# A four-layer encoder trunk on one core: the on-chip buffers get new addresses

## The chip, the core and the metric

One core of a Trainium2 chip runs the whole kernel. TensorE (PE) multiplies and writes to PSUM, VectorE (DVE), ScalarE (ACT) and GpSimd (POOL) do the rest, and SyncE's queue (SP) issues the transfers from HBM into SBUF, the on-chip memory of 128 partitions in which every tile lies at one byte address in each partition. The metric is the device time of one execution in microseconds. The kernel before takes 2548.47 us (median of 3 runs, 2547.91 to 2550.18).

## The reference

Input is x of 512 frames by 1024 features in float32. Four layers follow (FoX attention, mLSTM, gMLP, FoX), each with a SwiGLU behind it, and a last RMSNorm.

```python
def swiglu(h, w_gu, w_down):
    g, u = jnp.split(h @ w_gu, 2, axis=-1)
    return (jax.nn.silu(g) * u) @ w_down

def reference(x, norm1_g, norm2_g, final_g, ...):
    for i in range(DEPTH):
        kind, j = i % N_MIXERS, i // N_MIXERS
        hn = rmsnorm(x, norm1_g[i])
        if kind == 0:
            y = forgetting_attention(hn, a_w_in[j], a_b_f[j], a_w_out[j])
        elif kind == 1:
            y = mlstm_mixer(hn, ...)
        else:
            y = gmlp_mixer(hn, ...)
        x = x + y
        x = x + swiglu(rmsnorm(x, norm2_g[i]), ffn_w_gu[i], ffn_w_down[i])
    return rmsnorm(x, final_g)
```

SwiGLU has 2816 inner features, 22 tiles of 128. FoX has 16 heads of 64 with softmax over all earlier frames, mLSTM 8 heads of 128 with a short convolution ahead of it, gMLP 2048 gated features.

## The kernel before

The residual stream stays in SBUF as eight tiles X[k] of 128 features by 512 frames. Each operand of a large product is split into an exact high and a low part in float32r (`split`, lines 119 and 120: ACT rounds to the high part, DVE takes the difference), and each product runs as three passes (`mm3`, lines 124 to 126): high weights by high input, high weights by low input, low weights by high input. Three such matmuls of 128x512 are called a triple here. The stationary operand is loaded anew for each matmul. In `dense` the 128x128 slice of the weights (wH, wL) is stationary and the activation tile moves through the array: h = x * g (hH, hL) for the gate and up products of SwiGLU and the q, k, o and u products of the mixers, the activations aH, aL for SwiGLU's down projection, and the mixers' results oH, oL for their output products (`out_steps`). In `quarter_steps` (lines 164 to 166) and `token_major` (343 to 345), which make v with frames on partitions, the weights move and h is stationary.

There are 1984 triples with h (1408 of SwiGLU, 576 of the mixers), 704 with a, and 320 with o (64 of each FoX, 64 of mLSTM, 128 of gMLP). SwiGLU goes through its 22 tiles in groups of 8, 8 and 6: two products with h for each tile, then eight down products with the group's activations. Nothing else is put between those products. In the mixers `weave` puts the steps of the products with h, v and the first output products between the small matmuls of the heads (scores s from kk and qq, transposes pt, products po); the last four o tiles of a mixer have their output product behind all heads, with nothing between.

Tiles are handed out by pools that lie one behind the other in SBUF, in the order in which they are opened, and a tag with a number of buffers goes round them; a new tile waits until the old one in its place has been read. Weights come in units of 128x1024 into raw (3 buffers) and are split into wH and wL (4 buffers each). Pools opened inside a stage (fox, mlstm, gmlp, swiglu) take the room behind the standing ones and give it back. The order of the instructions on each engine is made by the scheduler of the language, so it can shift with the pools.

Of the kernel before, what the change touches and what calls it, by code (L numbers as in the profile page):

```python
# [16 lines left out]
P = 128  # L17
S = 512
# [12 lines left out]
# columns of the packed per-partition constants  # L31
# [7 lines left out]
class Trunk:  # L39
    """The residual stream is kept feature-major, X[k] = [128 features, 512 frames]. Every  # L40
    large product runs as three float32r passes over exact high and low parts."""

    def __init__(self, ctx, tc, a, first_g, first_w):
# [3 lines left out]
        pool = lambda name, **kw: ctx.enter_context(tc.tile_pool(name=name, **kw))  # L47
        self.cp = pool("const", bufs=1)
        self.xp = pool("resid", bufs=1)
        self.hp = pool("hid", bufs=1)  # L50
        self.wp = pool("wts", bufs=4)
        self.np_ = pool("norm", bufs=1)
# [5 lines left out]
        # the first weights come in quarters, between the k-tiles of x  # L58
# [22 lines left out]
        # mask[q, 384 + k] = 0 where q >= k, else NEG, and 0 in the columns before  # L81
# [25 lines left out]
    def weights_tiles(self):  # L107
        return (self.wp.tile([P, 1024], F32, name=self.nm("raw"), tag="raw", bufs=3),
                self.wp.tile([P, 1024], F32R, name=self.nm("wH"), tag="wH", bufs=4),
                self.wp.tile([P, 1024], F32R, name=self.nm("wL"), tag="wL", bufs=4))  # L110

# [22 lines left out]
    def dense_steps(self, src, xs, done):  # L134
        """The same product as a list of steps, to be woven with other work."""
# [13 lines left out]
    def quarter_steps(self, src, done):  # L149
        """256 columns, frames on partitions: src [2][128, 4 k-tiles * 256]."""  # L150
# [21 lines left out]
    def out_steps(self, src, o, final=False):  # L172
        """X += (4 k-tiles of o, which fills by the time of emission) @ w."""
# [16 lines left out]
    def start(self, steps, product, at=KT - 2):  # L190
        """The first quarter of v, k-tile by k-tile as they come, and RMSNorm's sums."""
# [26 lines left out]
    def norm_k(self, k):  # L218
        """X[k] is final: its part of h (whole for the last norm) and its squares."""
        if self.next_g == C_GF:  # L220
            self.squares_k(k)
            self.hidden_k(k)
        else:
            self.hidden_k(k)
            self.squares_k(k)
# [18 lines left out]
    def squares_k(self, k, pool=None):  # L244
        """Sums of squares; with a pool for them, in two sums on two engines."""
# [48 lines left out]
    def swiglu(self, l):  # L294
        nc = self.nc
        with ExitStack() as es:
            fp = es.enter_context(self.tc.tile_pool(name="ffn", bufs=2, reuse_waits="tile"))
            for k0, kn in FGROUPS:
                acts = []
                for j in range(k0, k0 + kn):  # L300
# [17 lines left out]
                    hi = fp.tile([P, S], F32R, name=self.nm("aH"), tag="aH", bufs=10)  # L318
                    lo = fp.tile([P, S], F32R, name=self.nm("aL"), tag="aL", bufs=10)
# [9 lines left out]
    def token_major(self, src, then=None):  # L329
        """src [4 units][128, 2 k-tiles * 512]; returns 4 PSUM tiles [128 frames, 512]."""  # L330
# [17 lines left out]
    def logsig(self, y, t):  # L348
        """y = log_sigmoid(y) = min(y, 0) - ln(1 + exp(-|y|))"""
# [8 lines left out]
    def fox(self, j):  # L358
        with ExitStack() as es:
            pool = lambda name, **kw: es.enter_context(  # L360
                self.tc.tile_pool(name=name, reuse_waits="tile", **kw))
            kp = pool("a_keep", bufs=1)
# [32 lines left out]
            # steps a (scores, softmax) run two ahead of steps b (transpose), c (product with v)  # L395
# [26 lines left out]
    def fox_v(self, ps, b):  # L422
        """Per head 64 columns of the high part and 64 of the low (odd heads: low first)."""
# [11 lines left out]
    def fox_q(self, ps, h, c2):  # L435
        """Per head, plane 0: q high twice; plane 1: q low and the rows of the bias."""
# [20 lines left out]
    def fox_k(self, ps, h, c2):  # L457
        """Per head, plane 0: k high and low; plane 1: k high and the rows of the bias."""
# [4 lines left out]
        for hh in range(2):  # L463
            me = slice(64 * hh, 64 * hh + 64)
            other = slice(64 - 64 * hh, 128 - 64 * hh)
            kk = self.ap.tile([P, 2, S], F32R, name=self.nm("kk"), tag="kk", bufs=3)
# [11 lines left out]
    def fox_head(self, h, QK, V, O):  # L478
# [9 lines left out]
        def a(j):  # L488
# [6 lines left out]
            # p = -(s + mask), mx = -max(s + mask)  # L495
# [11 lines left out]
        def b(j):  # L507
            # th/tl [128 keys, key block, 2 query blocks]
# [11 lines left out]
        def c(jg):  # L520
# [11 lines left out]
            if jg == 1:  # L532
# [3 lines left out]
                # the low part's product has landed on the other head's rows  # L536
                nc.scalar.copy(out=out[me], in_=po[other])
                nc.vector.tensor_tensor(out=out[me], in0=po[me], in1=out[me], op=ALU.add)
                if hh == 1:
                    oh, ol = T([P, S], "oH", 8, F32R), T([P, S], "oL", 8, F32R)  # L540
                    self.split(out, oh, ol)
                    O[pair] = (oh, ol)
# [6 lines left out]
    def fox_gate_weights(self, j):  # L549
        """Rows 0-15 of the product are from the high part of w, rows 32-47 from the low."""  # L550
# [18 lines left out]
    def fox_gate(self, j, pf, c2):  # L569
        """c2 = the high and low parts of c = cumsum(log_sigmoid(f + b_f))."""  # L570
# [10 lines left out]
        # brings the table of Exp in before the first softmax needs it  # L581
# [7 lines left out]
    def mlstm(self):  # L589
        with ExitStack() as es:  # L590
            pool = lambda name, **kw: es.enter_context(
                self.tc.tile_pool(name=name, reuse_waits="tile", **kw))
            kp = pool("b_keep", bufs=1)
# [70 lines left out]
    def mlstm_qk(self, ps, m, scale):  # L664
        """Causal depthwise convolution over frames, then y * sigmoid(y)."""
# [401 lines left out]
```

## Time and profile before

| what | kernel before |
|---|---|
| median of 3 runs | 2548.47 us |
| profiled execution, span from first to last instruction | 2546.0 us |
| PE busy with matmuls | 2518.0 us (99%), 12156 instructions |
| PE weight loads | 2098.7 us (82%), beside the matmuls |
| DVE, ACT, POOL busy | 1383.8 us (54%), 1067.1 us (42%), 228.4 us (9%) |
| DMA | 226.00 MB, 89 GB/s |

The span is the profiled execution's own time from the first to the last instruction; the page gives no time around it, and the median of the runs lies 2.5 us above. Matmul durations overlap one another, since the array takes the next matmul before the last one has left it. What a matmul costs the engine is therefore the distance from its start to the next one's, and not the duration: 97 starts of line 124 over 65.3 us make 96 triples of 0.680 us, though each of the three matmuls lasts 0.39 us by the records.

### The profile page before, as it was taken

How to read it: one execution, taken by the hardware profiler on the slowest of the kernel's cores; microseconds unless marked ns; L12 is line 12 of the kernel's file. 1: busy time of each engine (PE TensorE's matmuls, PEld its weight loads, DVE VectorE, ACT ScalarE, POOL GpSimd, SP SyncE). 2: the span in 40 equal slices, each digit the busy share in tenths (PEclk: the TensorE clock that was granted, in tenths of full speed). 3: DMA queues.
4: the chain of work that ended last, by engine and by line, in shares of the span. 5: the costliest groups of instructions: out<-in, count | busy, mean ns of one | idle time of the engine just before them, and what ended most of it. 6: DMA issues, size and time to landing. Idle time of an engine off the chain costs nothing.

```text
span 2546.0 us, 31856 instructions
## 1 busy us (share of the span) xinstructions
PE 2518.0 (99%) x12156; PEld 2098.7 (82%) x12156; DVE 1383.8 (54%) x2202; ACT 1067.1 (42%) x1779; POOL 228.4 (9%) x369
## 2 busy tenths in 40 slices
PE   8999999999999999999999999999999999999998
PEld 7898888888888888888888888888888888888886
DVE  6777444435777754444537655434346777444443
ACT  7776322223766642222333324222236776322222
POOL 2222100001000110000100001000002222000001
PEclk9999999999999999999999999999999999999999
DMA  4112332323222223232322222333232222232321
GB/s 144 59 61 76 96 94 98 92 96 97 67 75 84 83 91 99 92 100 89 109 91 91 92 83 97 94 100 92 98 92 77 67 69 75 91 95 96 100 85 64
DMA packets 69416, 226.00 MB, mean 89 GB/s; under 512 B 11793, under 2 KB 12817, under 8 KB 69265
## 3 DMA queue, kind: packets, MB, share of 16 engines
q1 hardware_dynamic: 69264, 223.98, 27.5%
q8 instruction: 96, 1.57, 0.3%
q14 instruction: 56, 0.45, 0.1%
HBM read 221.55 MB, written 2.10 MB: 88 GB/s over the span
## 4 chain that ended last, share of the span: by engine, by line
PE 95%; DVE 2%; ACT 1%; issue 1%; POOL 0%; DMA 0%; SPq 0%; DVEq 0%; POOLq 0%; ACTq 0%
PE acc L124 26%; PE acc L126 26%; PE acc L125 26%; PE acc L164 2%; PE acc L165 2%; PE acc L166 2%; PE pt L516 1%; PE acc L343 1%; PE acc L345 1%; PE acc L344 1%; PE po L531 1%; PE s L494 1%; PE po L530 1%; PE s L493 1%; PE po L737 0%
## 5 line engine op out<-in xcount | busy, mean ns | idle before, releaser
L119 ACT CAST wH<-raw 128x1024 fp32r<-128x1024 f32 (+2 forms) x427 | 439.3, 1030 | 1134.4 <-PE acc L125 1001.1
L124 PE MATMUL acc<-hH,wH 128*128 128x512 f32 x1984 | 784.8, 396 | 0.0
L126 PE MATMUL acc<-hH,wL 128*128 128x512 f32 x1984 | 774.1, 390 | 0.0
L125 PE MATMUL acc<-hL,wH 128*128 128x512 f32 x1984 | 773.6, 390 | 0.0
L120 DVE TENSOR_TENSOR wL<-raw,wH 128x1024 fp32r<-128x1024 f32 (+2 forms) x427 | 510.3, 1195 | 117.0 <-ACT wH L119 95.1
L126 PEld LDWEIGHTS acc<-hH,wL 128*128 128x128 f32 x1984 | 372.6, 188 | 79.8
L124 PEld LDWEIGHTS acc<-hH,wH 128*128 128x128 f32 x1984 | 373.1, 188 | 73.7 <-issue 0.5
L125 PEld LDWEIGHTS acc<-hL,wH 128*128 128x128 f32 x1984 | 373.2, 188 | 72.0 <-issue 0.2
L213 DVE TENSOR_TENSOR X<-acc,X 128x512 f32<-128x512 f32 x176 | 121.5, 690 | 299.3 <-PE acc L126 298.7
L126 PE MATMUL acc<-aH,wL 128*128 128x512 f32 x704 | 280.2, 398 | 0.0
L125 PE MATMUL acc<-aL,wH 128*128 128x512 f32 x704 | 278.0, 395 | 0.0
L124 PE MATMUL acc<-aH,wH 128*128 128x512 f32 x704 | 275.7, 393 | 0.0
L262 POOL TENSOR_TENSOR ssum<-ssum,sq 128x512 f32<-128x512 f32 x51 | 80.0, 1569 | 1628.1 <-ACT sq L257 1628.0
L316 DVE TENSOR_TENSOR u<-acc,rbc 128x512 f32<-128x512 f32 x88 | 60.8, 691 | 281.8 <-PE acc L126 281.8
L312 DVE TENSOR_TENSOR g<-acc,rbc 128x512 f32<-128x512 f32 x88 | 60.8, 691 | 188.4 <-PE acc L126 188.4
L125 PEld LDWEIGHTS acc<-aL,wH 128*128 128x128 f32 x704 | 132.1, 188 | 34.2 <-DVE aL L120 0.7
L124 PEld LDWEIGHTS acc<-aH,wH 128*128 128x128 f32 x704 | 132.2, 188 | 32.0
L126 PEld LDWEIGHTS acc<-aH,wL 128*128 128x128 f32 x704 | 132.2, 188 | 30.4
L124 PE MATMUL acc<-oH,wH 128*128 128x512 f32 x320 | 130.0, 407 | 0.1
L126 PE MATMUL acc<-oH,wL 128*128 128x512 f32 x320 | 126.5, 395 | 0.0
L125 PE MATMUL acc<-oL,wH 128*128 128x512 f32 x320 | 126.3, 395 | 0.0
L164 PE MATMUL acc<-wH,hH 128*128 128x256 f32 x384 | 116.2, 303 | 5.9 <-ACT hH L239 5.9
(217 smaller groups left out, 3056.4 us busy)
## 6 DMA issues: line engine op xcount, KB each, us to landing
raw<-in_w_g SPq DMA_DIRECT2D x88, 512.0 KB, 3.3
raw<-in_w_u SPq DMA_DIRECT2D x88, 512.0 KB, 3.3
raw<-in_w_d SPq DMA_DIRECT2D x64, 512.0 KB, 3.5
raw<-in_w_d SPq DMA_DIRECT2D x32, 384.0 KB, 3.1
raw<-in_a_q SPq DMA_DIRECT2D x16, 512.0 KB, 3.9
raw<-in_a_k SPq DMA_DIRECT2D x16, 512.0 KB, 3.5
raw<-in_a_o SPq DMA_DIRECT2D x16, 512.0 KB, 3.3
raw<-in_b_qk SPq DMA_DIRECT2D x16, 512.0 KB, 3.3
```

Of the source, the lines that this page charges most:

```text
L119: self.nc.scalar.copy(out=hi, in_=src)
L120: self.nc.vector.tensor_tensor(out=lo, in0=src, in1=hi.bitcast(F32), op=ALU.subtract)
L124: mm(ps, lH, rH, start=first, stop=False)
L125: mm(ps, lH, rL, start=False, stop=False)
L126: mm(ps, lL, rH, start=False, stop=last)
L164: mm(ps, hh[:, t], wh[:, c], start=k == 0, stop=False)
L165: mm(ps, hh[:, t], wl[:, c], start=False, stop=False)
L166: mm(ps, hl[:, t], wh[:, c], start=False, stop=k == KT - 1)
L213: self.nc.vector.tensor_tensor(out=self.X[m], in0=ps, in1=self.X[m], op=ALU.add)
L262: eng.tensor_tensor(out=t, in0=t, in1=sq, op=ALU.add)
L312: nc.vector.tensor_tensor(out=g, in0=pg, in1=self.r, op=ALU.mult)
L316: nc.vector.tensor_tensor(out=u, in0=pu, in1=self.r, op=ALU.mult)
```

## The change

The program's instructions stay the same in number and shape; what changes is where tiles lie. Pools can be opened from the low or from the high end of SBUF (`side="right"`). After the constants come now h, a new pool "parts" with eight pairs mH, mL (`part_tiles`) that takes the place of SwiGLU's aH, aL (ten pairs before) and of the mixers' oH, oL (eight pairs each), then wH and wL, and, inside the mixers, kk of FoX or q of mLSTM. X, raw, the tiles of RMSNorm and SwiGLU's g, sg and u go to the high end. mLSTM's q and k parts (four buffers of one tag before) have two buffers each, and its gate weights gst take the two of k's low part. All comments were removed too.

Where the tiles lie in the built programs, in KiB from the start of a partition, and the remainder of the first byte by 64 (tiles are 2 or 4 KiB, so a tag's buffers have the same remainder):

| tile | before | by 64 | after | by 64 |
|---|---|---|---|---|
| hH, hL | 34.9 to 66.9 | 0 | 18.9 to 50.9 | 0 |
| aH, aL (after: mH, mL) | 129.0 to 169.0 | 32 | 50.9 to 82.9 | 0 |
| oH, oL of FoX (mH, mL) | 191.3 to 223.3 | 32 | 50.9 to 82.9 | 0 |
| oH, oL of mLSTM (mH, mL) | 190.8 to 222.8 | 0 | 50.9 to 82.9 | 0 |
| oH, oL of gMLP (mH, mL) | 182.5 to 214.5 | 0 | 50.9 to 82.9 | 0 |
| wH | 78.9 to 94.9 | 0 | 82.9 to 98.9 | 0 |
| wL | 94.9 to 110.9 | 0 | 98.9 to 114.9 | 0 |
| kk, FoX | 169.2 to 181.2 | 32 | 114.9 to 126.9 | 0 |
| qq, FoX | 157.2 to 169.2 | 32 | 167.1 to 179.1 | 0 |
| fst, gate weights of FoX | 125.0 | 32 | 134.9 | 0 |
| gst, gate weights of mLSTM | 125.3 to 133.3 | 32 | 135.2 to 139.2 | 0 |
| X | 18.9 to 34.9 | 0 | 208.0 to 224.0 | 32 |

The diff, cut to its core:

```diff
         self.cp = pool("const", bufs=1)
-        self.xp = pool("resid", bufs=1)
         self.hp = pool("hid", bufs=1)
+        self.mp = pool("parts", bufs=8)
         self.wp = pool("wts", bufs=4)
-        self.np_ = pool("norm", bufs=1)
+        self.xp = pool("resid", bufs=1, side="right")
+        self.rp = pool("raw", bufs=3, side="right")
+        self.np_ = pool("norm", bufs=1, side="right")
...
-        return (self.wp.tile([P, 1024], F32, name=self.nm("raw"), tag="raw", bufs=3),
+        return (self.rp.tile([P, 1024], F32, name=self.nm("raw"), tag="raw"),
...
+    def part_tiles(self):
+
+        return tuple(self.mp.tile([P, S], F32R, name=self.nm(t), tag=t) for t in ("mH", "mL"))
...
-            fp = es.enter_context(self.tc.tile_pool(name="ffn", bufs=2, reuse_waits="tile"))
+            fp = es.enter_context(self.tc.tile_pool(name="ffn", bufs=2, side="right",
+                                                    reuse_waits="tile"))
...
-                    hi = fp.tile([P, S], F32R, name=self.nm("aH"), tag="aH", bufs=10)
-                    lo = fp.tile([P, S], F32R, name=self.nm("aL"), tag="aL", bufs=10)
+                    hi, lo = self.part_tiles()
...
+            self.kkp = pool("a_k", bufs=3)
...
-            kk = self.ap.tile([P, 2, S], F32R, name=self.nm("kk"), tag="kk", bufs=3)
+            kk = self.kkp.tile([P, 2, S], F32R, name=self.nm("kk"), tag="kk")
...
-                    oh, ol = T([P, S], "oH", 8, F32R), T([P, S], "oL", 8, F32R)
+                    oh, ol = self.part_tiles()
...
+            self.qp = pool("b_q", bufs=2)
...
-        hi = qp.tile([P, S], F32R, name=self.nm("qkH"), tag="qkH", bufs=4)
-        lo = qp.tile([P, S], F32R, name=self.nm("qkL"), tag="qkL", bufs=4)
+        home, tag = (self.qp, "q") if m < BH else (qp, "k")
+        hi = home.tile([P, S], F32R, name=self.nm("qkH"), tag=tag + "H", bufs=2)
+        lo = home.tile([P, S], F32R, name=self.nm("qkL"), tag=tag + "L", bufs=2)
...
-            g = self.bp.tile([P, S], F32R, name=self.nm("gst"), tag="qkL", bufs=4)
+            g = self.bp.tile([P, S], F32R, name=self.nm("gst"), tag="kL")
...
-                oh = op.tile([P, S], F32R, name=self.nm("oH"), tag="oH")
-                ol = op.tile([P, S], F32R, name=self.nm("oL"), tag="oL")
+                oh, ol = self.part_tiles()
```

The order of the instructions moves only in the first 50 us or so on PE, DVE and ACT, and in a few memsets, small casts and small transfers at the later stage starts. On PE at the start of the first FoX, behind the first quarter of v, stand the broadcast of 1/rms to all partitions (ps from rcol), the first q product (acc from h and wH) and the forget gate's product (pf from h and the gate weights fst). Before:

```order
L287 MATMUL ps_350<-ident,rcol_287 128x128 x4
L124 MATMUL acc_380<-hH_121,wH_375 128x512
L565 MATMUL pf_333<-hH_121,fst_200 48x512
L566 MATMUL pf_333<-hL_122,fst_200 48x512
L565 MATMUL pf_333<-hH_127,fst_200 48x512
L566 MATMUL pf_333<-hL_128,fst_200 48x512
L565 MATMUL pf_333<-hH_133,fst_200 48x512
```

After:

```order
L574 MATMUL pf_342<-hL_160,fst_209 48x512
L573 MATMUL pf_342<-hH_163,fst_209 48x512
L574 MATMUL pf_342<-hL_164,fst_209 48x512
L294 MATMUL ps_359<-ident,rcol_296 128x128 x4
L131 MATMUL acc_389<-hH_127,wH_384 128x512
L132 MATMUL acc_389<-hL_128,wH_384 128x512
L133 MATMUL acc_389<-hH_127,wL_385 128x512
L131 MATMUL acc_389<-hH_133,wH_384 128x512
```

The sixteen matmuls of the gate's product have moved ahead of the broadcast. On POOL at the same place, where ssum and sq are RMSNorm's sums of squares, rcol is 1/rms, and fst, fg, qq and kk are cleared for the gate and the heads, before:

```order
L84 AFFINE_SELECT mask<-mask 128x128
L262 TENSOR_TENSOR ssum_161<-ssum_161,sq_163 128x512
L262 TENSOR_TENSOR ssum_161<-ssum_161,sq_166 128x512
L262 TENSOR_TENSOR ssum_161<-ssum_161,sq_169 128x512
L557 MEMSET fst_200 128x384
L574 MEMSET fg_359 16x512
L281 TENSOR_TENSOR rcol_287<-ms_285,mhalf 128x4
L446 MEMSET qq_407 4x512
```

After:

```order
L86 MEMSET mask 128x512
L565 MEMSET fst_209 128x384
L87 AFFINE_SELECT mask<-mask 128x128
L582 MEMSET fg_368 16x512
L454 MEMSET qq_416 4x512
L269 TENSOR_TENSOR ssum_167<-ssum_167,sq_169 128x512
L454 MEMSET qq_423 4x512
L269 TENSOR_TENSOR ssum_167<-ssum_167,sq_172 128x512
L454 MEMSET qq_546 4x512
L269 TENSOR_TENSOR ssum_167<-ssum_167,sq_175 128x512
L475 MEMSET kk_463 4x512
L288 TENSOR_TENSOR rcol_296<-ms_294,mhalf 128x4
```

The clears of fst, fg and three qq, and one of kk, have moved ahead of rcol, those of fst, fg and of one qq ahead of the first sum.

## Rows read from the trace of the kernel before

**Rows 1.** The page: busy time and share by engine; granted clock; DMA queue.

```profile
PE 2518.0 (99%) x12156; PEld 2098.7 (82%) x12156; DVE 1383.8 (54%) x2202; ACT 1067.1 (42%) x1779; POOL 228.4 (9%) x369
...
PEclk9999999999999999999999999999999999999999
...
q1 hardware_dynamic: 69264, 223.98, 27.5%
```

**Rows 2.** The page: chain that ended last, shares by engine.

```profile
PE 95%; DVE 2%; ACT 1%; issue 1%; POOL 0%; DMA 0%; SPq 0%; DVEq 0%; POOLq 0%; ACTq 0%
```

**Rows 3.** The page, costliest groups: line, operation, tiles, shape, count | busy us, mean ns.

```profile
L124 PE MATMUL acc<-hH,wH 128*128 128x512 f32 x1984 | 784.8, 396 | 0.0
...
L124 PE MATMUL acc<-aH,wH 128*128 128x512 f32 x704 | 275.7, 393 | 0.0
...
L124 PE MATMUL acc<-oH,wH 128*128 128x512 f32 x320 | 130.0, 407 | 0.1
```

**Rows 4.** Line 124 in 280 to 345 us: count: duration min/median/max, first and last start.

```profile
L124 PE MATMUL acc<-hH,wH x97: 389/389/389, 279.7 to 345.0; 128*128 128x512 f32 x97
```

**Rows 5.** Line 343 in the whole span, same columns: weights are the moving operand.

```profile
L343 PE MATMUL acc<-wH,hH x128: 389/389/486, 1266.8 to 1355.1; 128*128 128x512 f32 x128
```

**Rows 6.** Timeline of PE (start us, us, engine, line): a gate triple and the next.

```profile
300.11 0.39 PE L124 MATMUL acc<-hH,wH 128*128 128x512 f32 x1
...
300.79 0.39 PE L124 MATMUL acc<-hH,wH 128*128 128x512 f32 x1
```

**Rows 7.** Timeline of PE: one triple of a down projection and the next start.

```profile
360.20 0.39 PE L124 MATMUL acc<-aH,wH 128*128 128x512 f32 x1
360.43 0.39 PE L125 MATMUL acc<-aL,wH 128*128 128x512 f32 x1
360.67 0.40 PE L126 MATMUL acc<-aH,wL 128*128 128x512 f32 x1
360.90 0.39 PE L124 MATMUL acc<-aH,wH 128*128 128x512 f32 x1
```

**Rows 8.** Line 124 in 355 to 390 us, a down projection.

```profile
L124 PE MATMUL acc<-aH,wH x50: 392/392/392, 355.3 to 389.6; 128*128 128x512 f32 x50
```

**Rows 9.** Line 124 in 2502 to 2534 us, the last down projection.

```profile
L124 PE MATMUL acc<-aH,wH x39: 394/394/394, 2502.0 to 2528.6; 128*128 128x512 f32 x39
```

**Rows 10.** Line 124 in 244.6 to 263 us, end of the first FoX output product.

```profile
L124 PE MATMUL acc<-oH,wH x26: 392/392/392, 244.6 to 262.1; 128*128 128x512 f32 x26
```

**Rows 11.** Line 124 in 886 to 899 us, end of the mLSTM output product.

```profile
L124 PE MATMUL acc<-oH,wH x19: 390/392/404, 886.1 to 898.7; 128*128 128x512 f32 x19
```

**Rows 12.** Line 124 in 1534 to 1552 us, end of the gMLP output product.

```profile
L124 PE MATMUL acc<-oH,wH x25: 388/388/388, 1534.5 to 1550.9; 128*128 128x512 f32 x25
```

**Rows 13.** Timeline of PE in the mLSTM gate product, first and last pair.

```profile
639.83 0.39 PE L797 MATMUL pg<-hH,gst 128*128 128x512 f32 x1
640.06 0.40 PE L798 MATMUL pg<-hL,gst 128*128 128x512 f32 x1
...
643.11 0.39 PE L797 MATMUL pg<-hH,gst 128*128 128x512 f32 x1
```

**Rows 14.** Timeline of PE among the FoX heads: four starts apart.

```profile
125.94 0.40 PE L125 MATMUL acc<-hL,wH 128*128 128x512 f32 x1
...
126.88 0.40 PE L124 MATMUL acc<-hH,wH 128*128 128x512 f32 x1
```

**Rows 15.** Timeline of PE at the start: [idle before <-releaser] ends a row.

```profile
23.48 0.28 PE L166 MATMUL acc<-wH,hL 128*128 128x256 f32 x1
25.11 2.07 PE L287 MATMUL ps<-ident,rcol 128*128 128x128 f32 x8 [1.35 <-POOL rcol L281]
27.02 0.77 PE L124 MATMUL acc<-hH,wH 128*128 128x512 f32 x1
27.58 0.63 PE L565 MATMUL pf<-hH,fst 128*48 128x512 f32 x1
...
31.55 0.39 PE L125 MATMUL acc<-hL,wH 128*128 128x512 f32 x1
```

**Rows 16.** Timeline of POOL at the start: two clears behind rcol.

```profile
25.11 0.98 POOL L446 MEMSET qq<- 4x512 f32 x2
```

More of the change, by code (lines that the diff above doesn't have):

```diff
@@ L698, in decay @@
         def decay():
-            mrow = T([2, S], "mrow", 2, F32R)
+            mrow = self.qp.tile([2, S], F32R, name=self.nm("mrow"), tag="mrow")
             for x in range(2):
@@ L768, in turn @@
                 op0=ALU.mult, op1=ALU.mult)
-            oh, ol = T([P, S], "oH", 8, F32R), T([P, S], "oL", 8, F32R)
+            oh, ol = self.part_tiles()
             self.split(sig, oh, ol)
@@ L853, in gmlp @@
             sp = es.enter_context(self.tc.tile_pool(name="c_s", bufs=2, reuse_waits="tile"))
-            op = es.enter_context(self.tc.tile_pool(name="c_o", bufs=8, reuse_waits="tile"))
             ps_s = es.enter_context(self.tc.tile_pool(name="c_ps", bufs=2, space=PSUM, reuse_waits="tile"))
@@ L870, in gmlp @@
                     self.rms_rows()
-            ws = self.wp.tile([P, 8, P], F32, name="ws", tag="raw", bufs=3)
+            ws = self.rp.tile([P, 8, P], F32, name="ws", tag="raw")
             nc.sync.dma_start(out=ws, in_=self.a["c_ws"])
@@ L939, in gate @@
                                         op=ALU.mult)
-                oh = op.tile([P, S], F32R, name=self.nm("oH"), tag="oH")
-                ol = op.tile([P, S], F32R, name=self.nm("oL"), tag="oL")
+                oh, ol = self.part_tiles()
                 self.split(u, oh, ol)
```

## The prediction

> **What bounds the kernel now.** I read the page first: PE is busy 99% of the span of 2546.0 us at the full granted clock (nines in every slice), DVE 54%, ACT 42%, the DMA queue 27.5% [rows 1]; the chain that ended last is 95% PE [rows 2]. So the kernel is a queue of matmuls, and what counts is the distance from one start to the next. I read it from lines with the first and last start and a count, in stretches where nothing is put between the matmuls, and compared it with where the moving operand lies (the table of places in the section on the change). With h moving, 97 starts of line 124 take 345.0 - 279.7 = 65.3 us: 96 triples of 0.680 us [rows 4, 6]. With wH and wL moving, 127 distances of line 343 take 88.3 us, 0.695 with the ends of stages in it, and its duration is the same 389 ns [rows 5]. With a moving, 49 triples take 34.3 us and 38 take 26.6 us: 0.700 us each, at 392 to 394 ns instead of 389 [rows 7 to 9]. With FoX's o, 25 triples take 17.5 us: 0.700 [rows 10]; mLSTM's, 18 in 12.6 us: 0.700, or 0.694 with the rounding at its favourable end [rows 11]; gMLP's, 24 in 16.4 us: 0.683, where rounding leaves 0.679 to 0.687 [rows 12]. The weights, PSUM's tiles and the order of the three matmuls are the same in all of them. What differs is the place of the moving tile: the quick ones lie below 111 KiB on a 64-byte boundary; the slow ones begin 32 bytes past one, or lie above 180 KiB, or both.
>
> **Two readings.** Either the height of the address costs time, or the start within 64 bytes does. The mLSTM gate product has h moving, low and even, and its stationary tiles gst at 125 KiB with remainder 32; 14 distances take 643.11 - 639.83 = 3.28 us, 0.234 each, as slow as a [rows 13]. So the stationary operand counts too, under either reading. After the change h, the parts, wH and wL all have remainder 0 and lie below 115 KiB, so both readings give the large products 0.680.
>
> **The change, part by part.** The instructions and their number stay.
> (1) Down projections: 704 triples [rows 3] by 0.700 - 0.680 = 0.020 us: 14.1 us less. They follow one another on PE without a gap, so all of it lies on the path.
> (2) Output products, 320 triples [rows 3]: FoX 128 by 0.020 = 2.6 us; mLSTM 64 by 0.016 (between 0.694 and 0.700) = 1.0; gMLP 128 by 0.007 (the upper end of its rounding, since its 388 ns are the nearest to 389) = 0.9. Together 4.5. About half of them are woven with head work, where I have no even stretch; if these kept their pace it would be 2.2.
> (3) Triples of h among head work, 576: a stretch among FoX's heads has four starts in 126.88 - 125.94 = 0.94 us, 0.235 each where h alone has 0.227, next to scores whose operands kk and qq have remainder 32 [rows 14]. At 0.008 for a matmul, 576 triples would give 13.8 us; this one stretch was picked right behind head matmuls, and farther from them h falls back to 0.227, so I bound the term by half of it, 6.9, and below by 0, since qq, the products' th, tl and vt and the identity stay high or uneven. I take 3.3, the middle.
> (4) The start: PE stands 1.35 us for rcol ahead of the broadcast [rows 15]. Now the gate's sixteen matmuls, 31.55 - 27.58 = 3.97 us, stand ahead of it and fill that time, and the clears on POOL are done while it waits for DVE. What is late next are the first scores, which wait for kk behind DVE's and ACT's splits, and they do not come sooner by as much. Between 0 and 1.4: I take 0.7. The one clear of kk that POOL now has ahead of rcol should end before the sums are there; if it does not, it delays rcol by its own 0.5 us [rows 16], so that loss is in the range.
> (5) Eight parts for ten: SwiGLU's ninth activation takes the place of its first, last read by the eighth down product. Its own gate and up products stand behind that on PE, 48 matmuls or 48 by 0.227 = 10.9 us, and its split can't start before they end, so the wait is free; the cover would have to shrink by all 10.9 us. The same holds where a mixer's o takes a place of the last down projection, and for gst in the two buffers of k's low part: head 0's k product stands behind the gate's product.
> (6) The small transfers for gate weights and gMLP's constants go out some places sooner on SP's queue, ahead of weight units; at 27.5% of the DMA engines' time nothing waits for those. DVE and ACT tiles at the high end may be slower to reach; at 54% and 42% a few ns for each of their instructions disappear behind PE.
> Sum: 14.1 + 4.5 + 3.3 + 0.7 = 22.6 us off the span: 2523.4. The span lies 2.5 us under the median of the runs, so 2525.9, **2526 us**. By the terms' ends it is 2519 (14.1 + 4.5 + 6.9 + 1.4 = 26.9 less, 2521.6, and 2 us for rounding in the distances) to 2533 (14.1 + 2.2 + 0 - 0.5 = 15.8 less).
>
> **A rule against it.** The a rows show 0.233 us from start to start of a 128x512 matmul where the h rows show 0.227 [rows 4, 8]. The Trainium skill, "TensorE: Matmul & The Clock Gate", section "Back-to-back issue gap", gives the warm gap as the column count over 2.4 plus 2.5 ns, 215.8 ns here, with no term for where an operand lies. By it, (1) to (3) are nothing; the trace has both values above its figure and apart from each other, so it doesn't agree.
>
> **The rivals.**
> A: place does nothing, and the pace of a stage comes from something that goes with the stage: how its PSUM tiles are emptied (one DVE addition in down products, three operations in gate and up), or a rhythm between weight loads and matmuls that each stage falls into. Then only the start moves: 2548.5 less 0 to 1.4, 2547.5. For it: the o products have three different paces. Against it: FoX's output product and SwiGLU's down projection are unlike in length and neighbours and have the same 0.700, and gMLP's, emptied in the same way, does not [rows 8, 10, 12]. 8%. This is also the case that the change doesn't do what its words say. The rule of the Trainium skill above would end here.
> B: height counts, also for the stationary operand, and the step lies just above 111 KiB, the highest place that was quick before. Then the last of wL's four buffers, now at 110.9 to 114.9 KiB, is over it: a quarter of 1984 + 704 + 320 = 3008 triples, 752, by up to 0.020 us as in rows 8, gives back up to 15.0 us, at least 752 by 0.007 (one matmul of three, 0.234 - 0.227 [rows 13]) = 5.3. So 2526 + 10 = 2536, between 2531 and 2541. For it: gst at 125 KiB is slow as stationary. Against it: its remainder explains that too. 10%.
> C, slower than before: h moves down to 18.9 KiB, where no moving operand of 512 columns was seen. If reads there were slow, the place is every triple of h, and the price 1984 by x. It decides from x = 22.6/1984 = 0.0114 us for a triple; at the 0.020 of a, 39.7 us: 2526 + 39.7 = 2566. For it: nothing but the gap in what was seen. Against it: from 35 to 111 KiB the pace is flat [rows 4, 5]. 4%.
>
> **How the numbers follow.** The forecast has the remaining 78%. Its own range is 2519 to 2533. Rival B mostly adds 2533 to 2538; A, C and the rest of B, some 15%, stay outside: 2519 to 2538. A measurement of this kernel can tell about 0.2%, 5.1 us. Faster by more than that are the forecast and B, 0.88; within it A with a little of C, 0.08; slower the rest of C, 0.04.
>
> **What would show it.** In the profile after, line 131 (124 before) with mH moving should have its starts 0.680 us apart in down projections and in the output products' ends; the gate product pf should stand at about 23.6 us with no idle time ahead of the broadcast; h triples behind scores should be nearer to 0.227 for a matmul. A down triple at 0.700 proves A; triples that are slow for one unit of weights in four prove B; gate and up at 0.69 or more prove C. The forecast fails if the pace of (1) doesn't change, and it is off by up to 4 us if (3) is at one of its ends.

## The result and the profile after

The kernel after takes 2529.12 us (median of 5 runs, 2527.86 to 2530.04) where the kernel before took 2548.92 in the same call (5 runs, 2547.91 to 2550.18): ratio 0.992, 95% interval 0.9908 to 0.9932, 19.8 us less. The forecast was 2526. The profiled span goes from 2546.0 to 2526.2 us, 19.8 less as well.

The page of the kernel after, busy us by engine, the granted clock and the shares of the chain that ended last, beside [rows 1, 2]:

```profile
PE 2498.8 (99%) x12156; PEld 2098.5 (83%) x12156; DVE 1382.9 (55%) x2202; ACT 1065.9 (42%) x1779; POOL 228.0 (9%) x369
...
PEclk9999999999999999999999999999999999999998
...
PE 95%; ACT 2%; DVE 2%; issue 1%; POOL 0%; DMA 0%; SPq 0%; DVEq 0%; POOLq 0%; ACTq 0%
```

The number of instructions is the same on each engine and only PE's busy time changes by more than 1.2 us. It is still a queue of matmuls. Line 131 of the kernel after (124 before), in five stretches: two down projections, then the ends of the output products of FoX, mLSTM and gMLP; count, duration in ns, first and last start:

```profile
L131 PE MATMUL acc<-mH,wH x62: 389/389/389, 349.1 to 390.6; 128*128 128x512 f32 x62
...
L131 PE MATMUL acc<-mH,wH x37: 389/389/389, 2481.3 to 2505.7; 128*128 128x512 f32 x37
...
L131 PE MATMUL acc<-mH,wH x25: 389/389/389, 242.5 to 258.9; 128*128 128x512 f32 x25
...
L131 PE MATMUL acc<-mH,wH x26: 389/389/389, 876.7 to 893.7; 128*128 128x512 f32 x26
...
L131 PE MATMUL acc<-mH,wH x23: 389/389/389, 1521.5 to 1536.4; 128*128 128x512 f32 x23
```

61 triples in 41.5 us, 36 in 24.4, 24 in 16.4, 25 in 17.0, 22 in 14.9: 0.680 us each to the rounding, where [rows 8 to 11] had 0.700 and [rows 12] 0.683.

The start changed too. Both kernels by stretch (us; PE busy and its instructions, PEld, DVE, ACT, POOL, granted clock, DMA share, GB/s), before:

```profile
23.70:25.10 1.40, 0.06 (x1) 0.00 (x0) 0.47 (x1) 0.01 (x1) 1.35 (x1) 0.89 0.00 0
25.10:27.00 1.90, 1.89 (x8) 1.79 (x9) 1.35 (x6) 1.90 (x8) 1.89 (x5) 0.50 0.76 276
27.00:28.00 1.00, 1.00 (x3) 0.56 (x3) 1.00 (x5) 0.90 (x3) 0.96 (x3) 0.50 0.00 0
```

and after:

```profile
23.60:25.10 1.50, 1.50 (x9) 0.84 (x8) 1.50 (x2) 0.01 (x1) 1.45 (x1) 1.00 0.00 0
25.10:27.30 2.20, 2.20 (x11) 1.18 (x10) 1.85 (x7) 1.90 (x7) 0.98 (x2) 1.00 0.83 259
27.30:28.10 0.80, 0.80 (x9) 0.79 (x8) 0.80 (x3) 0.58 (x1) 0.00 (x0) 1.00 0.88 312
```

Before, PE stands 1.35 us for rcol [rows 15] and then works at a granted clock of 0.50, the 1.2 GHz level, until about 28.2. After, the gate's product fills that time and the clock is at 1.00, the 2.4 GHz level. The broadcast begins at 27.31 and the first q product at 28.12; it used to begin at 27.02, but the gate's product stood behind its first matmul.

The kernel after has a stretch at 0.50 too, only sooner, from about 15.5 to 18.8 us; it begins while PE waits 1.29 us for DVE:

```profile
15.60:18.40 2.80, 2.68 (x12) 2.68 (x13) 2.80 (x4) 2.80 (x7) 2.23 (x3) 0.50 0.43 170
```

A second execution of the same kernel (experiment 9) waits 1.31 us at that place and stays at 1.00 all through the start; its first score begins at 43.84 us, here at 43.88. So a stretch at the lower clock is not a mark of one kernel.

What the first score waits for in both kernels is kk, the end of a chain on DVE and ACT that comes from the gate. DVE's product of the gate and 1/rms and its split of kk, before and then after:

```profile
33.07 0.68 DVE L577 TENSOR_TENSOR fg<-fg,rbc 16x512 f32<-16x512 f32 x1
...
45.45 1.41 DVE L470 TENSOR_TENSOR kk<-k,kk 64x512 fp32r<-64x512 f32 x2
...
30.69 0.67 DVE L585 TENSOR_TENSOR fg<-fg,rbc 16x512 f32<-16x512 f32 x1
...
43.14 1.40 DVE L478 TENSOR_TENSOR kk<-k,kk 64x512 fp32r<-64x512 f32 x2
```

From one to the other are 12.38 and 12.45 us: the chain begins 2.4 us sooner and takes as long as before.

Where the 19.8 us of the span went, by distances from each matmul's start to the next, summed by moving operand: a part 13.6 (493.0 to 479.4), output parts 3.3 (229.6 to 226.3), the start 1.9 (the first score begins at 43.88 us, before at 46.19; the first output product, when the heads are nearly done, at 203.28, before at 205.22). h behind that point is 1.9 quicker, 1.3 of it among gMLP's work. At the end this execution lost 1.0: from the first sum of the last norm to its broadcast PE took 5.8 us instead of 4.8, with the granted clock at 0.50 between 2511 and 2513 us, where the kernel before had 1.00 at the same work.

### The profile page after: what moved, and what is told of

Same layout as the page of the kernel before. It is cut to its first block, busy times and chain, and to the rows that moved or that the text cites. A ratio compares the mean times of both kernels' runs of the same rounds, so it can differ in the third digit from the quotient of the medians.

```text
span 2526.2 us, 31856 instructions
## 1 busy us (share of the span) xinstructions
PE 2498.8 (99%) x12156; PEld 2098.5 (83%) x12156; DVE 1382.9 (55%) x2202; ACT 1065.9 (42%) x1779; POOL 228.0 (9%) x369
## 4 chain that ended last, share of the span: by engine, by line
PE 95%; ACT 2%; DVE 2%; issue 1%; POOL 0%; DMA 0%; SPq 0%; DVEq 0%; POOLq 0%; ACTq 0%
PE acc L131 26%; PE acc L133 26%; PE acc L132 26%; PE acc L171 2%; PE acc L173 2%; PE acc L172 2%; PE pt L524 1%; PE acc L350 1%; PE acc L351 1%; PE acc L352 1%; PE po L539 1%; PE s L502 1%; PE s L501 1%; PE po L538 1%; PE ps L927 0%
## 5 line engine op out<-in xcount | busy, mean ns | idle before, releaser
L131 PE MATMUL acc<-mH,wH 128*128 128x512 f32 x1024 | 402.2, 394 | 0.2
L132 PE MATMUL acc<-mL,wH 128*128 128x512 f32 x1024 | 399.3, 390 | 0.0
L133 PE MATMUL acc<-mH,wL 128*128 128x512 f32 x1024 | 399.3, 390 | 0.0
L133 PEld LDWEIGHTS acc<-mH,wL 128*128 128x128 f32 x1024 | 192.2, 188 | 39.7
L131 PEld LDWEIGHTS acc<-mH,wH 128*128 128x128 f32 x1024 | 192.3, 188 | 39.3 <-ACT mH L126 1.5
L132 PEld LDWEIGHTS acc<-mL,wH 128*128 128x128 f32 x1024 | 192.5, 188 | 38.8 <-DVE mL L127 1.5
L173 PE MATMUL acc<-wH,hL 128*128 128x256 f32 x384 | 110.1, 287 | 1.3 <-DVE hL L247 1.3
L172 PE MATMUL acc<-wL,hH 128*128 128x256 f32 x384 | 109.5, 285 | 0.3 <-DVE wL L127 0.3
L512 POOL TENSOR_SCALAR p<-p,sm 128x128 f32<-128x128 f32 (+3 forms) x128 | 71.6, 560 | 306.8 <-DVE sm L511 298.8
```

The costliest lines, as they stand in the source:

```text
L131: mm(ps, lH, rH, start=first, stop=False)
L132: mm(ps, lH, rL, start=False, stop=False)
L133: mm(ps, lL, rH, start=False, stop=last)
L172: mm(ps, hh[:, t], wl[:, c], start=False, stop=False)
L173: mm(ps, hl[:, t], wh[:, c], start=False, stop=k == KT - 1)
L512: nc.gpsimd.tensor_scalar(out=p[:, :n], in0=p[:, :n], scalar1=sm, scalar2=0.0, op0=ALU.mult, op1=ALU.add)
```

## The experiments

Three theories stood at the beginning: **height** of the address, **start within 64 bytes** (the prediction's two readings), and its rival A, **pace of the stage**, by which place does nothing. Four kernels ran first. Experiments 1 to 6 are one run each.

**1. TensorE alone.** A kernel without the model; a run is a row of matmuls on two alternating slices:

```python
for i in range(N):
    nc.tensor.matmul(ps, stationary(i % 2), moving(i % 2), start=i == 0, stop=i == N - 1)
```

> The model is left out (x is only copied to the output); what is left is TensorE alone, in runs of 96 matmuls of 128x512 float32r with no wait between them. First set: the moving operand comes from 24 slots of 8 KiB, from 23 to 215 KiB of a partition, the stationary one lies at 16 KiB. Second set: the stationary operand comes from the slots, the moving one lies at 17 KiB. Third and fourth: moving, then stationary from the slots at 31 and at 103 KiB, at element offsets 0, 1, 2, 4, 8, 12, 16, 24 (8 and 24 leave 32 bytes over a multiple of 64). All slots begin on a multiple of 64 bytes. Theory 'height': in the first set one matmul takes 226.7 ns (a third of 0.680) up to some slot between 81 and 129 KiB and more from there, towards 233.3 ns (a third of 0.700); the third set is flat at 31 KiB. If height counts for the stationary operand too, the second set has the same step, but above 111 KiB. Theory 'start within 64 bytes': the first two sets are flat at 226.7 ns, and in the third the offsets 8 and 24 take 233.3 ns at either height. Rival 'the pace belongs to the stage, not to the place': every run takes the same.

The lowest, a middle and the highest slot (23, 111 and 207 KiB), first as moving, then as stationary operand; w and m lie low; columns as above:

```profile
L34 PE MATMUL ps<-sa,w x96: 388/389/390, 47.3 to 68.8; 128*128 128x512 f32 x96
L34 PE MATMUL ps<-m,sa x96: 388/389/390, 569.5 to 591.1; 128*128 128x512 f32 x96
...
L34 PE MATMUL ps<-sl,w x96: 388/389/390, 286.7 to 308.2; 128*128 128x512 f32 x96
...
L34 PE MATMUL ps<-sx,w x96: 388/389/390, 547.8 to 569.3; 128*128 128x512 f32 x96
L34 PE MATMUL ps<-m,sx x96: 388/389/390, 1070.0 to 1091.5; 128*128 128x512 f32 x96
```

95 distances in 21.5 us each: 226.7 ns in all 48 runs, so height costs nothing for either operand. The third and fourth sets were not flat: offsets of 1, 2, 4, 8, 12, 16, 24 elements gave 236.7, 231.6, 231.7, 233.3, 233.2, 228.9, 233.4 ns for the moving operand, the same at 31 and at 103 KiB, and 230.7 to 234.3 for the stationary one. Offsets other than 8 and 24 are slow too, 64 bytes among them: so not by the rule of the second theory either. Place within a small range does matter.

**2. Everything 32 bytes on**, in the kernel after:

```diff
+        pad = cp.tile([P, 8], F32, name="pad")
+        nc.gpsimd.memset(pad, 0.0)
         self.next_g = first_g
```

> The kernel after with 32 bytes of padding behind the constants: split h, the parts and the split weights stay as low as before, to 32 bytes, but all now begin 32 bytes over a multiple of 64. Theory 'height': triples stay at 0.680 us everywhere, time 2529 us. Theory 'start within 64 bytes': every triple goes to 0.700 as the down projections' did in the kernel before, 3008 triples by 0.020 = 60 us more, 2589 us. Rival 'pace of the stage': 0.680, 2529 us.

2529.01 us. Line 133 (131 before the padding) in a down projection, 56 triples in 38.0 us, 0.680 to the rounding:

```profile
L133 PE MATMUL acc<-mH,wH x57: 388/389/390, 351.8 to 389.8; 128*128 128x512 f32 x57
```

All large operands now have the remainder 32 that a had before, and none is slow. "Start within 64 bytes" falls.

**3. Parts to the top**, in the kernel after (with 32 bytes at the very top, so that the remainder stays 0):

```diff
-        self.mp = pool("parts", bufs=8)
+        self.mp = pool("parts", bufs=8, side="right")
```

> The kernel after with the pool of parts moved to the top (192 to 224 KiB, still on a multiple of 64); everything else that was low moves down by 32 KiB, the mixers' small operands too. Theory 'height': the 704 triples of the down projections and the output products' go back to 0.700, 14 to 20 us more, less up to 4 us that the mixers' small operands give back from their lower places: 2539 to 2549 us. Theory 'start within 64 bytes': triples stay at 0.680, 2525 to 2529 us. Rival 'pace of the stage' (the eight shared buffers, not the place, made the gain): 0.680 too, 2529 us.

2528.95 us, and 0.680 in the same down projection: 60 triples in 40.8 us. Height falls in the kernel as it fell alone.

```profile
L134 PE MATMUL acc<-mH,wH x61: 389/389/389, 349.7 to 390.5; 128*128 128x512 f32 x61
```

**4. The activations of the kernel before on a multiple of 64:**

```diff
+            pad = fp.tile([P, 8], F32, name=self.nm("pad"), tag="pad", bufs=1)
+            nc.gpsimd.memset(pad, 0.0)
             for k0, kn in FGROUPS:
```

> The kernel before with 32 bytes of padding at the head of the feed-forward pool: the activation parts stay at 129 to 169 KiB but now begin on a multiple of 64 bytes; nothing else moves. Theory 'height': the down projections' triples stay at 0.700 us, time 2548.9 us. Theory 'start within 64 bytes': they go to 0.680, 704 by 0.020 = 14.1 us less, 2534.8 us. Rival 'pace of the stage': 0.700, 2548.9 us.

2549.28 us; 48 triples in 33.6 us, 0.700, now with an uneven rhythm of 392 to 399 ns:

```profile
L124 PE MATMUL acc<-aH,wH x49: 392/397/399, 355.9 to 389.5; 128*128 128x512 f32 x49
```

This run also bears on the start. PE stands 1.34 us ahead of the broadcast as in the kernel before, but here the granted clock stays at 1.00 behind it; the stretch at 0.50 lay at 16.6 to 19.8 us:

```profile
25.60:27.50 1.90, 1.16 (x8) 0.97 (x9) 1.34 (x6) 1.90 (x8) 1.88 (x5) 1.00 0.78 276
```

Its first score begins at 46.17 us, no sooner than the 46.19 of the kernel before: PE now waits 0.75 us for DVE's vt where it worked slowly there.

By times alone this run spoke for height or for the stage, and experiment 3 against height. What all four have in common is seen by subtraction: in experiments 2 and 3, as in the kernel after, h, the parts and the weights lie multiples of 256 bytes **from one another**; a in the kernel before lay 96 bytes off the weights modulo 256, in experiment 4 128 off. So a fourth theory: **distance** between the starts of the moving and the stationary operand. It was put to the test in three runs.

**5. TensorE alone, by distance.**

```python
for d in range(0, 2049, 32):
    run((d, d), (0, 0))          # the moving operand d bytes on
for d in (4, 16, 32, 64, 128, 256, 416):
    run((d, d), (d, d))          # both d bytes on
```

> The model is left out again (x is only copied to the output). Runs of 64 matmuls, alternating two slices as before: (1) the moving operand begins 0, 32, 64 ... 2048 bytes further on, the stationary one stays; (2) both begin the same number of bytes further on (4, 16, 32, 64, 128, 256, 416); (3) the stationary one alone (32, 64, 128, 256, 384, 480, 512); (4) of two alternating pairs, either each matmul's own operands are 0 apart and the next one's stationary operand is d off its moving one, or the other way round, d being 32, 128, 256; (5) 128, 256 and 384 columns at distances 0, 32, 256. Theory 'distance': what counts is the distance between the start of the moving operand and that of the stationary one, taken modulo some power of two of 512 or less. Then (1) shows 226.7 ns at 0, 512, 1024, 1536, 2048 (oftener if the period is shorter) and 229 to 237 ns between, (2) is 226.7 ns all through, (3) is slow but for 512. Within it, 'the operand that is being loaded for the next matmul': in (4) the first kind is slow and the second fast; 'the matmul's own operands': the reverse. Theory 'start of each operand by itself, modulo more than 64': (2) is slow like (1). Rival 'pace of the stage': everything 226.7 ns.

One copy on DVE ends each run of 64, so the distance between two copies is 64 matmuls. Timeline of DVE: start us, us, engine, line. The first copy ends a run at 0; then come 0, 32, 64, 96, 128, 160, 192, 224, 256 bytes:

```profile
20.95 0.69 DVE L34 COPY sink<-ps 128x512 f32<-128x512 f32 x1 [20.95 <-PE ps L32]
35.45 0.69 DVE L34 COPY sink<-ps 128x512 f32<-128x512 f32 x1 [13.81 <-PE ps L32]
50.39 0.69 DVE L34 COPY sink<-ps 128x512 f32<-128x512 f32 x1 [14.24 <-PE ps L32]
65.05 0.69 DVE L34 COPY sink<-ps 128x512 f32<-128x512 f32 x1 [13.97 <-PE ps L32]
79.98 0.69 DVE L34 COPY sink<-ps 128x512 f32<-128x512 f32 x1 [14.24 <-PE ps L32]
94.91 0.69 DVE L34 COPY sink<-ps 128x512 f32<-128x512 f32 x1 [14.24 <-PE ps L32]
109.90 0.69 DVE L34 COPY sink<-ps 128x512 f32<-128x512 f32 x1 [14.30 <-PE ps L32]
124.84 0.69 DVE L34 COPY sink<-ps 128x512 f32<-128x512 f32 x1 [14.25 <-PE ps L32]
139.77 0.69 DVE L34 COPY sink<-ps 128x512 f32<-128x512 f32 x1 [14.24 <-PE ps L32]
154.30 0.69 DVE L34 COPY sink<-ps 128x512 f32<-128x512 f32 x1 [13.84 <-PE ps L32]
```

14.50 us at 0, 14.94 at 32, 14.66 at 64, 14.93 to 14.99 from 96 to 224, 14.53 at 256. The row repeats every 256 bytes up to 2048. Both operands moved together by 4, 16, 32, 64, 128 bytes, same view:

```profile
986.24 0.69 DVE L34 COPY sink<-ps 128x512 f32<-128x512 f32 x1 [13.85 <-PE ps L32]
1001.18 0.69 DVE L34 COPY sink<-ps 128x512 f32<-128x512 f32 x1 [14.26 <-PE ps L32]
1016.10 0.69 DVE L34 COPY sink<-ps 128x512 f32<-128x512 f32 x1 [14.23 <-PE ps L32]
1030.66 0.69 DVE L34 COPY sink<-ps 128x512 f32<-128x512 f32 x1 [13.86 <-PE ps L32]
1045.19 0.69 DVE L34 COPY sink<-ps 128x512 f32<-128x512 f32 x1 [13.84 <-PE ps L32]
1059.74 0.69 DVE L34 COPY sink<-ps 128x512 f32<-128x512 f32 x1 [13.86 <-PE ps L32]
```

From 32 bytes on they are quick (14.53 to 14.56), so it is the distance and not either start; at 4 and 16 bytes they are slow (14.94, 14.92), which the theory had not expected: a start that is no multiple of 32 costs by itself. With the stationary operand moved alone (the third set) the pace is 233.2 ns at 32 bytes, 233.4 at 64 and 480, 232.4 at 128 and 384, and 226.7 at 256 as at 512. So 64 bytes are nearly cheap only when the moving operand is the one that lies further on; the other way they count as 192. The fourth set stays undecided: 232.0 and 228.4 ns with own distance 0 and the next one's at 32 and 128, 230.0 with the reverse. Neither pair alone is the cause. With 384 columns the pace is 173.3 to 173.5 ns at the three distances tried, with 256 columns it is 120 at 0 and 118 at 32, with 128 columns 111 to 112: the cost was seen at 512 columns only.

The distances modulo 256 of the kernels, beside this map:

| moving operand | distance | triple in the kernel, us | three matmuls alone, us |
|---|---|---|---|
| all large ones, after | 0 | 0.680 | 3 x 226.7 = 0.680 |
| gMLP's o, before [rows 12] | 64 | 0.683 (0.679 to 0.687) | 3 x 228.9 = 0.687 |
| a and FoX's o, before [rows 7 to 10] | 96 | 0.700 | 3 x 233.4 = 0.700 |
| mLSTM's o, before [rows 11] | 128 | 0.694 to 0.700 | 3 x 233.3 = 0.700 |
| a, experiment 4 | 128 | 0.700 | 3 x 233.3 = 0.700 |

**6. The kernel after with the weights 32 bytes on:**

```diff
         self.mp = pool("parts", bufs=8)
+        self.padp = pool("pad", bufs=1)
+        pad = self.padp.tile([P, 8], F32, name="pad")
+        nc.gpsimd.memset(pad, 0.0)
         self.wp = pool("wts", bufs=4)
```

> The kernel after with 32 bytes of padding between the parts and the split weights; heights stay as they are. Theory 'distance': split h and the parts now lie 32 bytes off the weights, modulo 512, everywhere, so all 3008 triples go from 0.680 to about 0.700 us: 60 us more, and 2 to 3 us for the products in which the weights move: 2589 to 2593 us. 'Height', 'start within 64 bytes' (which fell for every operand moved by 32 bytes at once) and 'pace of the stage': no change, 2529 us.

2578.82 us, 49.7 more than the kernel after. Gate and up, then a down projection:

```profile
L134 PE MATMUL acc<-hH,wH x93: 395/396/396, 280.1 to 344.5; 128*128 128x512 f32 x93
...
L134 PE MATMUL acc<-mH,wH x61: 395/395/396, 353.6 to 395.6; 128*128 128x512 f32 x61
```

92 triples in 64.4 us and 60 in 42.0: 0.700 for h as well, which was never slow in either kernel. The 60 us of the expectation took all 3008 triples; the 1784 of h and 934 of the parts that another triple follows went from 1223.2 to 1255.5 and from 638.5 to 655.7 us, 49.5 together. The 290 that stand directly ahead of other work took only 0.8 more; why is not shown. The products in which the weights move are slower at 512 columns as well (381 distances, 227.2 to 233.8 ns each), but those with 256 columns are quicker, so that all of them together take 0.6 us more and not 2 to 3.

**7. The kernel before, every pool and height kept, matched by padding:**

```diff
+            pad = fp.tile([P, 104], F32, name=self.nm("pad"), tag="pad", bufs=1)
+            nc.gpsimd.memset(pad, 0.0)
             for k0, kn in FGROUPS:
...
+                    if not pair:
+                        nc.gpsimd.memset(T([P, 40], "pad", 1), 0.0)
                     oh, ol = T([P, S], "oH", 8, F32R), T([P, S], "oL", 8, F32R)
```

(and 32 and 112 elements likewise ahead of mLSTM's and gMLP's oH)

> The kernel before, all pools and heights as they were, with four tiles of padding: 416 bytes at the head of the feed-forward pool, 160, 128 and 448 bytes ahead of the output parts of the three mixers, so that the activation parts and the output parts begin a multiple of 512 bytes from the split weights; they were 96, 352, 384 and 64 off. Theory 'distance': the down projections' triples go from 0.700 to 0.680 (704 by 0.020 = 14.1 us) and the output products' lose the 2.7 us that they lost in the kernel after: 2532 us, ratio 0.993, without any operand having been moved to a lower address. Rival 'height' and rival 'pace of the stage, the shared pool of eight': triples stay at 0.700, 2548.9 us.

2531.13 us against 2549.01 on the same chip (ratio 0.9929, 0.9912 to 0.9945). A down projection, FoX's and mLSTM's output product:

```profile
L124 PE MATMUL acc<-aH,wH x63: 389/389/389, 351.8 to 393.9; 128*128 128x512 f32 x63
...
L124 PE MATMUL acc<-oH,wH x24: 389/389/389, 245.9 to 261.5; 128*128 128x512 f32 x24
...
L124 PE MATMUL acc<-oH,wH x29: 389/389/389, 879.8 to 898.9; 128*128 128x512 f32 x29
```

0.680 in all: at 129 and at 191 KiB, with ten buffers and own pools. By the sums of distances a takes 479.4 us and the output parts 226.1, as in the kernel after (the 2.7 us of the expectation are 3.3 there). Four tiles of padding make 17.9 of the gain, and no operand had to go low. What this kernel lacks against the kernel after is the start: it still stands 1.34 us ahead of the broadcast, and its first score begins at 46.91 us.

**8. The kernel after with the mixers' small operands matched too**, and **9.** the kernel after once more:

```diff
-            mx, sm = T([P, 1], "mx", 4), T([P, 1], "sm", 4)
+            mx, sm = T([P, 1], "mx", 8), T([P, 1], "sm", 8)
...
-        fst = fst.rearrange("p a b -> p (a b)")[:, 0:KT * 48].rearrange("p (k h) -> p k h", h=48)
+        fst = fst.rearrange("p a b -> p (a b)")[:, 0:KT * 64].rearrange("p (k h) -> p k h", h=64)[:, :, 0:48]
```

(and 160 and 32 bytes of padding in mLSTM's and gMLP's pools; twice four small buffers of 32 bytes move the queries and tl by 128 and 256)

> The kernel after, with the operands of the mixers' own products (the queries and the probabilities' low parts of the forgetting attention, its gate weights, the keys and decayed weights of the mLSTM, the gated half of the gMLP) also moved, by 32 to 160 bytes of padding, so that they begin a multiple of 256 bytes from split h and the parts. Theory 'distance': the pairs of the kernel after whose distance is not 0 modulo 256 are over 226.7 ns by about 1.3 us in sum; 1.3 us less, 2527.8 us, with a product of h that is followed by the queries' load near 227 ns instead of 235. That is less than this measurement can tell, so the rows decide. Rival 'what is left among head work is waits, not pace': rows and time unchanged, 2529.1 us.

> The kernel after, unchanged, beside the kernel with the mixers' operands matched, on the same chip: 2529.1 us, ratio 0.992 to the kernel before. What theory 'distance' gives the other kernel should be the difference to this run.

2527.01 us (0.9916, 0.9902 to 0.9929) beside 2528.16 (0.992, 0.9906 to 0.9933): 1.15 less, which the intervals do not tell from nothing. In the rows it shows. The stretch of [rows 14] in the kernel after, where the queries lie 128 bytes off:

```profile
123.96 0.40 PE L132 MATMUL acc<-hL,wH 128*128 128x512 f32 x1
124.19 0.40 PE L133 MATMUL acc<-hH,wL 128*128 128x512 f32 x1
124.43 0.40 PE L501 MATMUL s<-kk,qq 128*128 128x512 f32 x1
...
124.90 0.40 PE L131 MATMUL acc<-hH,wH 128*128 128x512 f32 x1
```

and in experiment 8:

```profile
123.76 0.39 PE L132 MATMUL acc<-hL,wH 128*128 128x512 f32 x1
123.99 0.39 PE L133 MATMUL acc<-hH,wL 128*128 128x512 f32 x1
124.22 0.40 PE L501 MATMUL s<-kk,qq 128*128 128x512 f32 x1
...
124.69 0.39 PE L131 MATMUL acc<-hH,wH 128*128 128x512 f32 x1
```

0.94 us for four starts, as before the change, and 0.93 now; the two distances behind h go from 0.23 and 0.24 to 0.23 and 0.23. Over the trace the 55 products of h ahead of a load of queries go from 235.3 to 230.9 ns, not to 227, and the 32 matmuls with fst, a quarter of them at distance 0 before and all of them now, go from 231.7 to 234.2. So part of what is left among head work follows distance and part doesn't, and why the latter is above 227 stays open. This is the kernel with the lowest median of all, by a margin that is not shown.

## Why the prediction came out

The time was right and the reason for most of it was wrong. That the h pace would pass to a and o held; neither of the two readings that were given for it did. So the number came out partly by luck: the new places met a condition that the prediction did not know of.

- **What bounds the kernel**: right. PE is busy 99% before and after, its busy time falls by 19.2 us (2518.0 to 2498.8), and the distances between its starts account for the 19.8 us of the span.
- **The two readings**: both fall (experiments 1 to 4). "h, the parts, wH and wL all have remainder 0 and lie below 115 KiB" is true and is not why; what counts is that pools of 2 and 4 KiB tiles now follow one another with nothing odd between, so their distances are multiples of 256. Before, three small tiles of the norm pool (ms and two of rcol, each taking 32 bytes) stood between the weights and a: its 96 bytes. The step that failed is the inference from a table by 64 bytes and by height: the two were looked at for each operand by itself, and never the difference of two operands, though the gate product with gst asked for it. It too fits: 160 bytes off, 0.234 [rows 13] as in the map; after, 0 off, 14 distances in 636.85 - 633.65 = 3.20 us, 0.229.
- **(1) Down projections**: 14.1 predicted, 13.6 measured, and shown by experiments 6 and 7.
- **(2) Output products**: 4.5 taken, 3.3 measured, about midway between that and the 2.2 of "if these kept their pace". The woven halves of FoX and mLSTM hardly gain, 0.4 us, where their even halves gain 1.6; gMLP's products gain 1.3. Among head work the load that comes next belongs to another operand; that this is the reason is not shown.
- **(3) h among head work**: 3.3 taken; the mixers' products with h are 0.9 quicker from the first score on, near the lower end. gMLP's gain 1.3, and 1.5 in experiment 7, where only the parts moved; those of the two FoX stages lose 0.5, 0.3 of it in one longer wait for POOL's p. The row behind the term was read as slow h; its slow distances were those next to the queries' load, whose distance the change moved from 32 to 128 bytes, no better: 232.2 ns before, 235.3 after.
- **(4) The start**: 0.7 taken, 2.3 measured at the first score, above the upper end. The gate's product begins at 23.61 us and no idle time stands ahead of the broadcast, as predicted. The step that failed is the bound: the term priced PE's idle 1.35 us, while the first score waits for the gate's chain on DVE and ACT. The last matmul of the gate's product starts at 27.09 us instead of 31.33, and with it DVE's product of the gate and 1/rms begins 2.4 us sooner. That PE worked at a granted clock of 0.50 behind the gap in the kernel before explains little of it: in experiment 4 the clock is 1.00 there and the first score comes no sooner. Its broadcast begins 0.5 us later, so by this estimate the clock's part is 0.5 us at most. All this is read from rows: no run moved the gate's product alone.
- **(5), (6)**: free, as said: no wait of PE behind the first score has grown by more than 0.3 us, none is on DMA, and the two on parts are under 0.1.
- Sum: 13.6 + 3.3 + 0.9 + 2.3 = 20.1 measured for (1) to (4), against 22.6; the span gave 19.8. (1), (2) and (3) were 4.1 us too large, (4) 1.6 too small, and errors of both signs met in the middle.
- **Rivals**: A falls with experiments 6 and 7, which change the pace of every stage by padding alone. B falls: no triple in four is slow with wL up to 114.9 KiB, and in experiment 1 a stationary operand at 207 KiB is as quick as at 23. C falls: h at 18.9 KiB takes 89 starts of line 131 from 279.7 to 339.6, 0.680.

On the rule that was weighed: the rows still go against it, 226.7 ns at the best distance and 233.3 at others. The Trainium skill, "TensorE: Matmul & The Clock Gate", section "Back-to-back issue gap", has 2.5 ns over the column count by 2.4, for a matmul by itself; for a row of float32r matmuls with their weight loads it is 13.3 by experiment 5, at 384 columns too (173.3). The Trainium skill, "SBUF — State Buffer", section "Operand start alignment", asks of an operand's start only that it is a multiple of its element size, and says that this is about legality, not speed. The results here don't contradict that, but the pace asks for more: multiples of 32 bytes, and 256 from one operand to the other.

## What to carry to other kernels

Where rows of the same matmul form differ by a few per cent, write down the addresses of both operands and subtract them; a table of each by itself misled here. Allocate what TensorE reads in tiles of multiples of 256 bytes one behind the other, and small odd tiles behind them: four pads were worth 0.7% on a kernel that is all matmul. And what closing a gap of PE is worth is read from the chain that ends last behind it, here the gate's on DVE and ACT, not from the gap's length; a second execution tells whether a stretch at the lower clock belongs to the kernel.

## What the runs showed of the hardware

- A 128x512 float32r matmul with its weight load follows the last one after 226.7 ns when moving and stationary operand start a multiple of 256 bytes apart, after 229 when the moving one lies 64 bytes further on modulo 256, and 232 to 234 at other multiples of 32. At 384, 256 and 128 columns a distance of 32 bytes cost under 1 ns (only 0, 32 and 256 were tried).
- Height in SBUF changes nothing for either operand: 226.7 ns in slots that begin at 23 to 207 KiB.
- Starts off a multiple of 32 bytes (4 and 16 were tried) take 233.5 and 233.2 ns even if both operands share the offset.
- The granted clock at the start fell to 0.50 for some 3 us in some executions: in the kernel before from 24.8 to 28.2 us, in a gap of 1.35 us of PE, and in the kernel after from 15.5 to 18.8, in a gap of 1.29. In the second execution of the kernel after it stayed at 1.00 with a gap of 1.31 at the same place, and in experiment 4 with a gap of 1.34 ahead of the broadcast. What decides it is not shown.
- Not settled: which distance counts, that of a matmul's own operands or that to the next one's load (230 to 232 ns for either alone at 32 bytes), and why products with fst, a stationary operand of 48 columns, stay at 234 at distance 0 in experiment 8.
